# Half-range Fourier sums, one silu activation and accumulated weight sums in a gated attention block

## The chip, the cores and the metric

The kernel runs on one core of a Trainium2 chip. A NeuronCore has TensorE (PE, matrix products), VectorE (DVE), ScalarE (ACT), GpSimd (POOL) and SyncE (SP); every engine runs its own instructions in order and they wait for each other by semaphores. The metric is device time in microseconds: the median over the runs shown. For the kernel before, three runs gave a median of 1290.94 us (1290.84 to 1290.96).

## The reference

One layer over 512 latent tokens of width 2048, with 256 context tokens. The input is normalised and modulated, one projection `h @ w_in` (2048 to 9216 columns) gives q, k, v, the gates and the Fourier branch, and two mixers run side by side: attention, and a Fourier mix over four groups of 128 channels. What the change touches is this:

```python
u_b = p_rest[..., R_UB:R_ZB]          # 512 tokens x 512 channels
z_b = p_rest[..., R_ZB:R_GA]
ug = u.astype(jnp.float32).reshape(b, n, N_FNET_GROUPS, FNET_GROUP)
y = jnp.fft.fftn(ug, axes=(1, 3), norm="ortho").real     # tokens and 128 channels of a group
y_b = (_fourier_mix(u_b) * jax.nn.silu(z_b)) @ w_pb
```

`norm="ortho"` divides by the root of 512 x 128, which is 256. The result is the real part of a two-dimensional transform: with A the token transform of a group, it is a sum over channels of cos times the real part of A and a sum over channels of sin times its imaginary part, for each of 512 token frequencies. Because `u` is real, frequency 512 - f of A is the conjugate of frequency f.

## The kernel before

**Stages.** Three stages matter here. The start stage projects the 1024 columns of `u_b` and `z_b` while the modulation vectors come in. The Fourier stage, a dozen microseconds long, mixes `u_b` and multiplies by silu(`z_b`) into the tile `part`. After it come eight groups of the large projection, written as Strassen-like products, seven products to a group and four pieces to a product (`PRODUCTS`, `stream_product`, `Group`). Attention, the two branch projections and the output projection follow.

**How an f32 product is done.** Each f32 operand is split into a high part, rounded to fp32r by an ACT copy (`split_from`, L180), and a low part, the difference, by a DVE subtraction (L181). `mm3` (L338 to L340) multiplies high by high, high by low and low by high.

**The Fourier stage.** `halves` folds the tokens so that even and odd frequencies need only 256 rows each. `tokens(g)` (L918) forms, for one group of channels, the token transform of the frequencies 0 to 256: two parts e (even and odd frequencies) of six matmuls with 258 and 256 columns, their sums in `bank()`, split into `ah` and `al`. `positions(g)` (L931) then transforms the channels: for two halves q of the 512 frequencies and for cos and sin (r), that is four steps, each with a product against the high and the low part of the table `fch` on `ah` and one against its high part on `al`. The second half reads the same columns backwards (`slice(256, 0, -1)`) with the other sign of sin, for which `fch` has a third block. One DVE instruction (L944) scales by 1/256 and multiplies by the gated z. `gate_b(g)` (L946) makes silu(z) before it: a sigmoid on ACT (L949) into a tile `e` of one buffer, and a DVE product (L950).

**Order.** In this stage PE's order is written out (`ordered`, a manual schedule): tokens 0, tokens 1, positions 0, tokens 2, positions 1, tokens 3, positions 2, positions 3, then the first group. The order of the other engines, POOL and SP included, is chosen by the tile framework from its own cost model as instructions become ready; between instructions that are ready, those written earlier in the program go first in the places looked at below. An exception is written out: the splits of the next pieces (`split_piece` at L961) come behind `low[g]`, the last low part of that group of channels, on DVE.

**PSUM.** The pool of the start and Fourier stages has eight banks: two by `bank3()` (banks 0 and 1, `pc` in the trace), two by `bank2()` (banks 2 and 3, `pd`), four by `bank()` (banks 4 to 7, `pb`). The pool of the groups takes their place: the first tile `x`, which product P1 of group 0 sums into, lies over banks 0 and 1. A tile of the new pool waits for the last reader of the banks below it.

**Weights of the groups.** A product multiplies a sum of weight blocks. `chain[pc]` (tiles R0 to R3, one for each piece) holds a running sum: product P1 uses block 0, Q5 block 0 plus block 1, Q6 that plus block 2, Q4 that plus block 3. A block is added in one of two ways. It can be loaded by SP into one of the raw buffers `wr` and be added by DVE (L268): the steps named in `BY_DVE_GATES`, here step 1, that is Q5's. Or POOL issues an accumulating transfer from DRAM onto the tile, after the split of the sum before (`nxt`, L291). The sum is split two to four pieces ahead of its use (`look`). A piece takes a raw buffer for each block that it loads; there are four, and two more from L890 on.

POOL's queue around the stage holds the two stores of `part` to `b_d` (L966), the second of which waits for the last group of channels, the load `qr<-rot_d` (L1394), which waits until both stores have landed, and then the accumulating transfers of group 0.

**Who reads `part`.** `b_d` is read back much later, in the attention stage.

Of the kernel before, what the change touches and what calls it, by code (L numbers as in the profile page):

```python
# [10 lines left out]
F32 = mybir.dt.float32  # L11
F32R = mybir.dt.float32r
ACT = mybir.ActivationFunctionType
ALU = mybir.AluOpType
# [4 lines left out]
P = 128  # L19
D = 2048  # L20
T = 512
# [23 lines left out]
RAW = 4  # L45

HL, MORE_HL = 3, 2
EVEN = 258

# [9 lines left out]
BY_DVE_GATES, BY_DVE_OUT = (1,), ()  # L61
# [61 lines left out]
def block_kernel(ctx, tc, xT, ctx_rows, ctx_toks, x, c_row, w_ss, w_gate, vecs, qkg, rope, dft_c, dft_s,  # L123
                 w_start, w_g, w_pab, w_o, final_g, out):
    nc = tc.nc
# [30 lines left out]
    def uid(s):  # L156
        cnt[0] += 1
        return f"{s}{cnt[0]}"
# [11 lines left out]
    def bank(shape=(P, 512)):  # L170
        return ps.tile(list(shape), F32, tag="b1", bufs=4, name=uid("pb"))

    def bank2():
        return ps.tile([P, 512], F32, tag="b2", bufs=2, name=uid("pd"))
# [4 lines left out]
    def split_from(src, hi, lo):  # L179
        first = nc.scalar.activation(hi, src, ACT.Copy)  # L180
        return first, nc.vector.tensor_tensor(lo, src, hi.bitcast(F32), op=ALU.subtract)  # L181
# [16 lines left out]
    def stream(key, src, *a, **k):  # L198
        todo.append(Piece(key, src if isinstance(src, list) else [src], *a, **k))
# [136 lines left out]
    def mm3(o, ah, al, bh, bl, start, stop, cont=False):  # L336

        nc.tensor.matmul(o, ah, bh, start=start, stop=False, skip_group_check=cont)  # L338
        nc.tensor.matmul(o, ah, bl, start=False, stop=False, skip_group_check=cont)  # L339
        nc.tensor.matmul(o, al, bh, start=False, stop=stop, skip_group_check=cont)  # L340
# [25 lines left out]

    for p in start_pieces():
        if p[2:5:2] == (KK - 4, 0):
            stream(("dfts", 0), dft_s[:, : 2 * EVEN], 2 * EVEN, 2, "raw")
            stream(("dftc", 0), dft_c, 3 * P, 1, "raw")  # L370
        elif p[2:5:2] == (KK - 4, 4):
            stream(("dfts", 1), dft_s[:, 2 * EVEN :], T, 2, "raw")
        stream(("start", p), w_start[p[0] : p[0] + P * p[1]].rearrange("(p c) -> p c", p=P), p[1], p[2 + 1])
    kept = {}

# [15 lines left out]
    def stream_product(name, g, w, by_dve, pieces=4):  # L391

        what = next(p[2] for p in PRODUCTS if p[0] == name)
        for pc in range(pieces):
            key = (name, g, pc)
            part = lambda i: w[CHAIN[i][0], CHAIN[i][1], pc]
            r = (pc + CHAIN_FROM.get(g, 0)) % 4
            if isinstance(what, tuple) and name == "P7" and g >= BRANCH_A:
                stream(key, [p7_d[g - BRANCH_A, pc]], 1024, 2, pc=r)
            elif isinstance(what, tuple):  # L400
                off = name == "P7"
                stream(key, [w[a, b, pc] for a, b in what], 1024, 2, pc=r, nxt=part(3) if off else None, off=off)
            else:
                stream(key, [part(what)] if what in by_dve else [], 1024, 2, stage=what, pc=r,
                       nxt=part(what + 1) if what < (3 if g >= BRANCH_A else 2) and what + 1 not in by_dve else None)
                todo[-1].first = part(0)
# [14 lines left out]
    for g in range(LAST + 1):  # L421
        for name in ONE_GROUP:
            if (g, name) == (LAST, "Q4"):
                stream_keys(0)
            if g == KV:
                f = CTX_FORMS.index(next(f for n, f, _, _ in PRODUCTS if n == name))
                stream(("cf", name), cf_d[:, :, f].rearrange("i p j c -> p i j c"), 1024, 8, dst=ctx_tiles)
            stream_product(name, g, w_g[g], BY_DVE_GATES)
            for pc in range(4):
                p = context_piece(g, name, pc)  # L430
                if p:
                    src, cols = (ctx_toks[p[1]], 1024) if p[0] == "cn" else (ctx_rows[p[1]], 4 * C)
                    stream(p, src, cols, 1, "raw")
                    todo.insert(len(todo) - 4 + pc, todo.pop())
            for pc in range(4):
                if (g, name, pc) in GATE_AT:
                    q = GATE_AT[g, name, pc]
                    stream(("gate", q), w_gate[q], 1024, 1, "raw")
                    e = todo.pop()
                    at = next(i for i, x in enumerate(todo) if x.key == (name, g, pc))  # L440
                    todo.insert(at + 1, e)
    for i in range(2):
        stream(("b", i), flat(b_d[i]), 1024, 2, dst=lambda: tiles("b"))
    q = NGATE
# [19 lines left out]
    pst, ppool = region("part", "right")  # L464
    part = ppool.tile([P, NS, T], F32, name="part")
# [47 lines left out]
    with tc.issue_after(nc.scalar.activation(ce, cvt, ACT.Exp, scale=-1.0).ins):  # L513
# [3 lines left out]
    nc.vector.tensor_tensor(c2[:, :, 0:2].rearrange("p k j -> p j k"),  # L517
                            cvt.rearrange("p (j k) -> p j k", j=2),
                            ce.rearrange("p (j k) -> p j k", j=2), op=ALU.mult)
    fch = ppool.tile([P, 2, 3 * P], F32R, name="fch")  # L520
    fsq = [ppool.tile([P, 2, 2, EVEN], F32R, name="fsq0")]
    rx = pap.tile([P, T], F32, name="rx")
    wacc = bank3()
    def warm(n, src):
# [251 lines left out]
    with tc.manual_schedule(engines={E.PE}):  # L776
# [6 lines left out]
        with tc.manual_schedule(engines={E.Activation, E.DVE}):  # L783
# [25 lines left out]
            for kb in range(1, 4):  # L809
                k = kb + 1  # L810
# [32 lines left out]
            for kb in range(4, KK - 4, 2):  # L843
# [6 lines left out]
                k = kb + 2  # L850
# [42 lines left out]
    fn, fnp = region("fn")  # L893
    uh = fnp.tile([P, 2, 2, T], F32R, name="uh")
    ul = fnp.tile([P, 2, 2, T], F32R, name="ul")
    fsq.append(fnp.tile([P, 2, 2, 256], F32R, name="fsq1"))
    split_table(1)

    def halves(a):
# [16 lines left out]
    AH, low = {}, {}  # L916

    def tokens(g):  # L918

        ah, al = (fnp.tile([P, 2, 257], F32R, tag=n, bufs=2, name=uid(n)) for n in ("ah", "al"))  # L920
        c = slice(P * g, P * g + P)
        for e in range(2):
            n = fsq[e].shape[-1]
            acc = bank()
            for a in range(2):
                mm3(acc[:, :n], uh[:, a, e, c], ul[:, a, e, c], fsq[e][:, 0, a, :], fsq[e][:, 1, a, :], a == 0, a == 1)
            k = slice(e, 257 - e, 2)
            low[g] = split_from(acc[:, :n].rearrange("p (r f) -> p r f", r=2), ah[:, :, k], al[:, :, k])[1]
        AH[g] = ah, al

    def positions(g):  # L931

        ah, al = AH.pop(g)
        acc = bank2()
        steps = [(256 * q, P * (r and 1 + q), (slice(0, 256) if q == 0 else slice(256, 0, -1)), r)
                 for q in range(2) for r in range(2)]
        for n, (o, t, k, r) in enumerate(steps):
            for m, i in enumerate((0, 1)):
                nc.tensor.matmul(acc[:, o : o + 256], fch[:, i, t : t + P], ah[:, r, k], start=n == m == 0, stop=False,
                                 skip_group_check=True)  # L940
        for n, (o, t, k, r) in enumerate(steps):
            nc.tensor.matmul(acc[:, o : o + 256], fch[:, 0, t : t + P], al[:, r, k], start=False, stop=n == 3,
                             skip_group_check=True)
        nc.vector.scalar_tensor_tensor(part[:, 4 + g, :], acc, 1.0 / 256.0, part[:, 4 + g, :], op0=ALU.mult, op1=ALU.mult)  # L944

    def gate_b(g):  # L946
        z = part[:, 4 + g, :]
        e = fnp.tile([P, T], F32, tag="sil", bufs=1, name=uid("e"))
        nc.scalar.activation(e, z, ACT.Sigmoid)  # L949
        nc.vector.tensor_tensor(z, z, e, op=ALU.mult)  # L950

    tokens(0)
    tokens(1)
# [724 lines left out]
    for i in range(NSTEP + 3):  # L1678
        h, t = divmod(i, 4)
# [20 lines left out]
        n = next((n for n, at in enumerate(SUM_AT) if at <= i < at + 3), None)  # L1700
# [8 lines left out]
        if i == 3:  # L1709
            with tc.issue_after(maxima[0].ins), tc.issue_after(maxima[1].ins):  # L1710
                e = take((1024,))
# [8 lines left out]
        if i in GATE_STEPS:  # L1720
            n = NGATE + GATE_STEPS.index(i)
# [267 lines left out]
def _constants():  # L1989
    pos = np.arange(T)  # L1990
    inv = (THETA ** (-np.arange(32, dtype=np.float64) / 32)).astype(np.float32)
    ang = np.stack([(pos // GRID).astype(np.float32)[:, None] * inv,
                    (pos % GRID).astype(np.float32)[:, None] * inv], axis=1)
    ang = ang.astype(np.float64)
    cos, sin = np.cos(ang), np.sin(ang)
    cos = np.stack([cos, cos], axis=2).reshape(T, HD)
    sin = np.stack([-sin, sin], axis=2).reshape(T, HD)
    rope = np.stack([cos, sin]).reshape(2, 4, P, HD).transpose(2, 0, 1, 3).astype(np.float32)
    a = 2 * np.pi * (np.outer(np.arange(P), np.arange(P)) % P) / P
    dft_c = np.concatenate([np.cos(a), -np.sin(a), np.sin(a)], axis=1).astype(np.float32)  # L2000

    def table(f):
        a = 2 * np.pi * (np.outer(np.arange(T // 2), f) % T) / T
        v = np.concatenate([np.cos(a), np.sin(a)], axis=1).astype(np.float32)
        return v.reshape(2, P, -1).transpose(1, 0, 2).reshape(P, -1)

    dft_s = np.concatenate([table(np.arange(0, T // 2 + 1, 2)), table(np.arange(1, T // 2, 2))], axis=1)
    return np.ascontiguousarray(rope), np.ascontiguousarray(dft_c), np.ascontiguousarray(dft_s)


# [58 lines left out]
```

## Time and profile before

| | |
|---|---|
| median of three runs | 1290.94 us |
| the profiled execution | 1290.61 us, of which the span of instructions is 1288.8 us |
| PE, DVE, ACT, POOL busy in the span | 1272.9, 994.7, 682.2, 170.8 us |
| Fourier stage on PE (first token matmul to P1's first) | 144.60 to 156.13 us |
| P1 of group 0 on PE, 48 matmuls | 156.13 to 167.02 us |
| mean granted TensorE clock | 0.998 |

The profile counts microseconds from the start of the span. A timeline row gives start, duration (us), engine, line, operation, output and inputs, shape and count, and in brackets how long the engine sat idle before it and what released it. Matmuls overlap: a row's duration is longer than the distance to the next row's start, and that distance is what a matmul costs. The same holds for DVE and ACT, where one instruction's start to the next one's is a little shorter than its duration. A row of the stretches gives its length and then each engine's busy time and instruction count, the granted clock, the DMA share and GB/s.

### The profile page before, as it was taken

How to read it: one execution, taken by the hardware profiler on the slowest of the kernel's cores; microseconds unless marked ns; L12 is line 12 of the kernel's file. 1: busy time of each engine (PE TensorE's matmuls, PEld its weight loads, DVE VectorE, ACT ScalarE, POOL GpSimd, SP SyncE). 2: the span in 40 equal slices, each digit the busy share in tenths (PEclk: the TensorE clock that was granted, in tenths of full speed). 3: DMA queues.
4: the chain of work that ended last, by engine and by line, in shares of the span. 5: the costliest groups of instructions: out<-in, count | busy, mean ns of one | idle time of the engine just before them, and what ended most of it. 6: DMA issues, size and time to landing. Idle time of an engine off the chain costs nothing.

```text
span 1288.8 us, 17680 instructions
## 1 busy us (share of the span) xinstructions
PE 1272.9 (99%) x6586; PEld 1047.9 (81%) x6586; DVE 994.7 (77%) x1305; ACT 682.2 (53%) x1073; POOL 170.8 (13%) x222
## 2 busy tenths in 40 slices
PE   8999999999999999999999999999999999999997
PEld 5677887888888888888888888888888888888886
DVE  5767899889779787658587666788898777887677
ACT  5322654645556555444355544666667646464544
POOL 0000011111102011012031010012100211211210
PEclk9999999999999999999999999999999999999999
DMA  9998588888988988977879897578852989998986
GB/s 378 408 369 344 208 216 248 237 218 261 227 302 236 301 269 260 291 197 184 278 207 259 286 249 237 182 245 241 270 178 75 249 244 258 244 211 229 225 200 179
DMA packets 104486, 319.14 MB, mean 248 GB/s; under 512 B 9904, under 2 KB 33072, under 8 KB 100432
## 3 DMA queue, kind: packets, MB, share of 16 engines
q1 hardware_dynamic: 55056, 197.40, 42.3%
q0 software_dynamic: 27024, 98.19, 35.6%
q10 hardware_dynamic: 22320, 22.42, 5.1%
q8 instruction: 51, 0.84, 0.3%
q14 instruction: 35, 0.29, 0.1%
HBM read 283.36 MB, written 34.61 MB: 247 GB/s over the span
## 4 chain that ended last, share of the span: by engine, by line
PE 91%; DVE 3%; DMA 2%; ACT 2%; issue 1%; SPq 0%; ACTq 0%; DVEq 0%
PE banks L338 10%; PE banks L339 10%; PE banks L340 10%; PE x L340 9%; PE x L338 9%; PE x L339 9%; PE y L340 7%; PE y L339 7%; PE y L338 7%; PE banks L1543 2%; PE pd L566 2%; PE pb L338 1%; PE pb L339 1%; PE pb L340 1%; PE pc L338 1%; DMA wa<-in_w_ss 1%
## 5 line engine op out<-in xcount | busy, mean ns | idle before, releaser
L180 ACT ACTIVATE whi<-R 128x1024 fp32r<-128x1024 f32 x138 | 145.6, 1060 | 142.1 <-PE banks L340 55.3
L181 DVE TENSOR_TENSOR wlo<-R,whi 128x1024 fp32r<-128x1024 f32 x138 | 167.9, 1222 | 57.9 <-ACT whi L180 57.6
L181 DVE TENSOR_TENSOR wlo<-wr,whi 128x1024 fp32r<-128x1024 f32 (+1 forms) x122 | 147.2, 1214 | 63.1 <-ACT whi L180 63.1
L180 ACT ACTIVATE whi<-wr 128x1024 fp32r<-128x1024 f32 (+1 forms) x122 | 127.4, 1052 | 127.3 <-PE y L340 44.3
L338 PE MATMUL banks<-whi,s 128*128 128x512 f32 (+1 forms) x400 | 157.8, 394 | 0.9 <-DVE ev L1106 0.9
L339 PE MATMUL banks<-wlo,s 128*128 128x512 f32 (+1 forms) x400 | 155.8, 389 | 0.0
L340 PE MATMUL banks<-whi,s 128*128 128x512 f32 (+1 forms) x400 | 155.8, 389 | 0.0
L338 PE MATMUL x<-whi,s 128*128 128x512 f32 x352 | 137.1, 390 | 0.0
L340 PE MATMUL x<-whi,s 128*128 128x512 f32 x352 | 137.0, 389 | 0.0
L339 PE MATMUL x<-wlo,s 128*128 128x512 f32 x352 | 136.9, 389 | 0.0
L338 PE MATMUL y<-whi,s 128*128 128x512 f32 x316 | 123.1, 389 | 0.2 <-DVE cxe L1266 0.2
L339 PE MATMUL y<-wlo,s 128*128 128x512 f32 x316 | 123.1, 390 | 0.0
L340 PE MATMUL y<-whi,s 128*128 128x512 f32 x316 | 122.8, 389 | 0.0
L291 POOL DMA_DIRECT2D R<-in_w_g x64 | 56.0, 875 | 415.2 <-DVE wlo L181 212.6
L180 ACT ACTIVATE s<-wr 128x512 fp32r<-128x512 f32 (+2 forms) x93 | 60.9, 678 | 68.1 <-DMA wr<-cf_d 24.9
L338 PEld LDWEIGHTS banks<-whi,s 128*128 128x128 f32 x400 | 75.2, 188 | 16.6 <-DVE ev L1106 1.3
L181 DVE TENSOR_TENSOR s<-wr,s 128x512 fp32r<-128x512 f32 (+2 forms) x93 | 66.7, 750 | 28.3 <-ACT s L180 27.5
L340 PEld LDWEIGHTS banks<-whi,s 128*128 128x128 f32 x400 | 75.1, 188 | 15.3
L339 PEld LDWEIGHTS banks<-wlo,s 128*128 128x128 f32 x400 | 75.2, 188 | 13.6 <-DVE wlo L181 0.2
L340 PEld LDWEIGHTS x<-whi,s 128*128 128x128 f32 x352 | 66.1, 188 | 13.8
L339 PEld LDWEIGHTS x<-wlo,s 128*128 128x128 f32 x352 | 66.1, 188 | 13.7
L338 PEld LDWEIGHTS x<-whi,s 128*128 128x128 f32 x352 | 66.1, 188 | 13.6
(322 smaller groups left out, 2803.2 us busy)
## 6 DMA issues: line engine op xcount, KB each, us to landing
wr<-in_w_g SPq DMA_DIRECT2D x128, 512.0 KB, 5.8
R<-in_w_g POOLq DMA_DIRECT2D x64, 512.0 KB, 7.3
wa<-in_w_ss SPq DMA_DIRECT2D x31, 1024.0 KB, 9.7
R<-in_w_g SPq DMA_DIRECT2D x32, 512.0 KB, 6.0
wr<-in_w_gate SPq DMA_DIRECT2D x32, 512.0 KB, 5.1
wr<-in_w_o SPq DMA_DIRECT2D x24, 512.0 KB, 7.5
R<-in_w_o POOLq DMA_DIRECT2D x24, 512.0 KB, 9.2
wr<-in_w_pab SPq DMA_DIRECT2D x20, 512.0 KB, 6.0
```

Of the source, the lines that this page charges most:

```text
L180: first = nc.scalar.activation(hi, src, ACT.Copy)
L181: return first, nc.vector.tensor_tensor(lo, src, hi.bitcast(F32), op=ALU.subtract)
L291: nc.gpsimd.dma_start(chain[e.pc], e.nxt, accum_op=ALU.add)
L338: nc.tensor.matmul(o, ah, bh, start=start, stop=False, skip_group_check=cont)
L339: nc.tensor.matmul(o, ah, bl, start=False, stop=False, skip_group_check=cont)
L340: nc.tensor.matmul(o, al, bh, start=False, stop=stop, skip_group_check=cont)
L566: nc.tensor.matmul(acc[32 * j : 32 * j + 32], c2[:, n, :], w[:, k, :], start=n < 4, stop=n >= KK - 4)
L1543: nc.tensor.transpose(tp[:, k * P : (k + 1) * P], p[:, k * P : (k + 1) * P], ident)
```

## The change

There are three edits.

1. `positions(g)` forms the cosine and the sine sum for frequencies 0 to 256 only (258 columns with a pad), each by one `mm3` into a bank of its own: cosine into `bank2()`, sine into `bank3()`. ACT copies the sine sum to SBUF (`odd`). DVE writes `y`: cosine minus sine for frequencies 0 to 256, cosine plus sine, read backwards, for 257 to 511; a third DVE instruction multiplies by z. The factor 1/256 goes into the table, whose third block goes. The odd frequencies' token table gets 258 columns as well, so `ah` and `al` are 258 wide. Six matmuls to a group of channels take the place of twelve, four instructions (one on ACT, three on DVE) the place of one.
2. `gate_b` is one ACT activation, `Silu`, in place. The DVE product L950 and the tile `e` go. Every later gate of the kernel still uses `Sigmoid` (L1182) or `Tanh` (L1224, L1357).
3. For group 0 alone, `by_dve` is empty: block 1 of Q5's four sums is not loaded into raw buffers and added by DVE, but added by four accumulating transfers, each issued by POOL after the split of P1's piece.

```diff
-    fch = ppool.tile([P, 2, 3 * P], F32R, name="fch")
+    fch = ppool.tile([P, 2, 2 * P], F32R, name="fch")
...
-            stream_product(name, g, w_g[g], BY_DVE_GATES)
+            stream_product(name, g, w_g[g], BY_DVE_GATES if g else ())
...
 def tokens(g):
-            n = fsq[e].shape[-1]
-            acc = bank()
+            acc = bank()[:, :FREQ]
...
 def positions(g):
-        acc = bank2()
-        steps = [(256 * q, P * (r and 1 + q), (slice(0, 256) if q == 0 else slice(256, 0, -1)), r)
-                 for q in range(2) for r in range(2)]
-        for n, (o, t, k, r) in enumerate(steps):
-            for m, i in enumerate((0, 1)):
-                nc.tensor.matmul(acc[:, o : o + 256], fch[:, i, t : t + P], ah[:, r, k], start=n == m == 0, stop=False,
-                                 skip_group_check=True)
-        for n, (o, t, k, r) in enumerate(steps):
-            nc.tensor.matmul(acc[:, o : o + 256], fch[:, 0, t : t + P], al[:, r, k], start=False, stop=n == 3,
-                             skip_group_check=True)
-        nc.vector.scalar_tensor_tensor(part[:, 4 + g, :], acc, 1.0 / 256.0, part[:, 4 + g, :], op0=ALU.mult, op1=ALU.mult)
+        acc = [b()[:, :FREQ] for b in (bank2, bank3)]
+        for r, o in enumerate(acc):
+            t = slice(P * r, P * r + P)
+            mm3(o, fch[:, 0, t], fch[:, 1, t], ah[:, r, :], al[:, r, :], True, True)
+        z = part[:, 4 + g, :]
+        y, odd = (fnp.tile([P, n], F32, tag=t, bufs=2, name=uid(t)) for t, n in (("y", T), ("odd", FREQ)))
+        nc.scalar.copy(odd, acc[1])
+        nc.vector.tensor_tensor(y[:, :257], acc[0][:, :257], odd[:, :257], op=ALU.subtract)
+        nc.vector.tensor_tensor(y[:, 257:], acc[0][:, 255:0:-1], odd[:, 255:0:-1], op=ALU.add)
+        nc.vector.tensor_tensor(z, y, z, op=ALU.mult)

     def gate_b(g):
         z = part[:, 4 + g, :]
-        e = fnp.tile([P, T], F32, tag="sil", bufs=1, name=uid("e"))
-        nc.scalar.activation(e, z, ACT.Sigmoid)
-        nc.vector.tensor_tensor(z, z, e, op=ALU.mult)
+        nc.scalar.activation(z, z, ACT.Silu)
...
-    dft_c = np.concatenate([np.cos(a), -np.sin(a), np.sin(a)], axis=1).astype(np.float32)
+    dft_c = (np.concatenate([np.cos(a), np.sin(a)], axis=1) / 256.0).astype(np.float32)
...
-    dft_s = np.concatenate([table(np.arange(0, T // 2 + 1, 2)), table(np.arange(1, T // 2, 2))], axis=1)
+    dft_s = np.concatenate([table(np.arange(e, FREQ, 2)) for e in range(2)], axis=1)
```

`FREQ` is the new name of `EVEN`, 258.

More of the change, by code (lines that the diff above doesn't have):

```diff
@@ L47 @@
 HL, MORE_HL = 3, 2
-EVEN = 258
+FREQ = 258
 FORMS = ("Z5", "S2", "S3", "S4")
@@ L368, in block_kernel @@
         if p[2:5:2] == (KK - 4, 0):
-            stream(("dfts", 0), dft_s[:, : 2 * EVEN], 2 * EVEN, 2, "raw")
-            stream(("dftc", 0), dft_c, 3 * P, 1, "raw")
+            stream(("dfts", 0), dft_s[:, : 2 * FREQ], 2 * FREQ, 2, "raw")
+            stream(("dftc", 0), dft_c, 2 * P, 1, "raw")
         elif p[2:5:2] == (KK - 4, 4):
-            stream(("dfts", 1), dft_s[:, 2 * EVEN :], T, 2, "raw")
+            stream(("dfts", 1), dft_s[:, 2 * FREQ :], 2 * FREQ, 2, "raw")
         stream(("start", p), w_start[p[0] : p[0] + P * p[1]].rearrange("(p c) -> p c", p=P), p[1], p[2 + 1])
@@ L519, in block_kernel @@
                             ce.rearrange("p (j k) -> p j k", j=2), op=ALU.mult)
-    fch = ppool.tile([P, 2, 3 * P], F32R, name="fch")
-    fsq = [ppool.tile([P, 2, 2, EVEN], F32R, name="fsq0")]
+    fch = ppool.tile([P, 2, 2 * P], F32R, name="fch")
+    fsq = [ppool.tile([P, 2, 2, FREQ], F32R, name="fsq0")]
     rx = pap.tile([P, T], F32, name="rx")
@@ L895, in block_kernel @@
     ul = fnp.tile([P, 2, 2, T], F32R, name="ul")
-    fsq.append(fnp.tile([P, 2, 2, 256], F32R, name="fsq1"))
+    fsq.append(fnp.tile([P, 2, 2, FREQ], F32R, name="fsq1"))
     split_table(1)
@@ L918, in tokens @@
     def tokens(g):
-        ah, al = (fnp.tile([P, 2, 257], F32R, tag=n, bufs=2, name=uid(n)) for n in ("ah", "al"))
+        ah, al = (fnp.tile([P, 2, FREQ], F32R, tag=n, bufs=2, name=uid(n)) for n in ("ah", "al"))
         c = slice(P * g, P * g + P)
         for e in range(2):
-            n = fsq[e].shape[-1]
-            acc = bank()
+            acc = bank()[:, :FREQ]
             for a in range(2):
-                mm3(acc[:, :n], uh[:, a, e, c], ul[:, a, e, c], fsq[e][:, 0, a, :], fsq[e][:, 1, a, :], a == 0, a == 1)
-            k = slice(e, 257 - e, 2)
-            low[g] = split_from(acc[:, :n].rearrange("p (r f) -> p r f", r=2), ah[:, :, k], al[:, :, k])[1]
+                mm3(acc, uh[:, a, e, c], ul[:, a, e, c], fsq[e][:, 0, a, :], fsq[e][:, 1, a, :], a == 0, a == 1)
+            k = slice(e, FREQ, 2)
+            low[g] = split_from(acc.rearrange("p (r f) -> p r f", r=2), ah[:, :, k], al[:, :, k])[1]
         AH[g] = ah, al
```

## The prediction

> **What bounds the kernel now.** The page's first section comes first, then the stretches around the edits, then PE's waits.
>
> ```profile
> PE 1272.9 (99%) x6586; PEld 1047.9 (81%) x6586; DVE 994.7 (77%) x1305; ACT 682.2 (53%) x1073; POOL 170.8 (13%) x222
> ```
>
> ```profile
> 144.60:156.13 11.53, 11.53 (x98) 11.53 (x96) 11.25 (x21) 8.51 (x16) 0.53 (x1) 1.00 0.20 79
> 156.13:184.00 27.87, 27.87 (x124) 22.82 (x123) 27.87 (x31) 16.46 (x19) 4.58 (x6) 1.00 0.88 247
> 184.00:212.00 28.00, 27.29 (x120) 22.27 (x120) 27.93 (x37) 14.41 (x32) 5.93 (x7) 1.00 0.71 170
> 420.00:500.00 80.00, 80.00 (x357) 66.29 (x356) 63.67 (x103) 44.16 (x64) 6.88 (x8) 1.00 0.89 281
> ```
>
> ```profile
> PE x L339 <- DVE s L181: 0.7, 1, 0.7
> PE y L340 <- DVE s L181: 0.2, 1, 0.2
> ```
>
> PE is the bound nearly everywhere, so time that PE gives up in one place is won at the end if nothing else is late afterwards. But from the Fourier stage to 212 us DVE has no idle time either: two bounds lie on top of each other, and PE's only waits in groups 0 and 1 are these two, 0.9 us, both on DVE. An edit that shortens PE alone there would be eaten by DVE; so both are summed.
>
> **Edit 1 on PE.** The stage's PE timeline:
>
> ```profile
> 144.60 0.28 PE L338 MATMUL pb<-fsq,uh 128*128 128x258 f32 x1
> 147.47 1.12 PE L939 MATMUL pd<-ah,fch 128*128 128x256 f32 x8
> 148.43 0.64 PE L942 MATMUL pd<-al,fch 128*128 128x256 f32 x4
> 148.91 0.28 PE L338 MATMUL pb<-fsq,uh 128*128 128x258 f32 x1
> 153.12 0.28 PE L340 MATMUL pb<-fsq,ul 128*128 128x256 f32 x1
> 153.24 1.12 PE L939 MATMUL pd<-ah,fch 128*128 128x256 f32 x8
> 155.64 0.65 PE L942 MATMUL pd<-al,fch 128*128 128x256 f32 x4
> 156.13 0.40 PE L338 MATMUL x<-whi,s 128*128 128x512 f32 x1
> 167.02 0.39 PE L338 MATMUL y<-whi,s 128*128 128x512 f32 x1
> ```
>
> Twelve position matmuls take 148.91 - 147.47 = 1.44 us, 0.12 each, whether 256 or 258 columns. Six fewer in each of four groups of channels are 24 x 0.12 = 2.88 us: by count P1 starts at 153.25. The two more columns in the odd tables cost under 0.02 us each time, taken as nothing.
>
> The stage can't keep that whole, because the sums must be split before they are used. The rows that set the pace:
>
> ```profile
> 153.44 0.41 ACT L180 ACTIVATE ah<-pb 128x256 fp32r<-128x256 f32 x1 [0.30 <-PE pb L340]
> 153.74 2.00 ACT L180 ACTIVATE s<-Z 128x1024 fp32r<-128x1024 f32 x2
> 148.53 1.22 DVE L181 TENSOR_TENSOR wlo<-R,whi 128x1024 fp32r<-128x1024 f32 x1
> 149.66 0.69 DVE L944 SCALAR_TENSOR_TENSOR part<-pd,part 128x512 f32<-128x512 f32 x1
> 150.27 0.43 DVE L181 TENSOR_TENSOR al<-pb,ah 128x258 fp32r<-128x258 f32 x1
> 150.62 0.68 DVE L950 TENSOR_TENSOR part<-part,e 128x512 f32<-128x512 f32 x1
> 151.22 0.42 DVE L181 TENSOR_TENSOR al<-pb,ah 128x256 fp32r<-128x256 f32 x1
> ```
>
> From the starts, DVE pays 1.13 us for a weight's low part, 0.35 for `al`, 0.60 for L944 or L950. The new instructions are not in the trace. The half-width subtraction and addition read PSUM and one SBUF tile, as `al` does: 0.35 each; the one read backwards could cost more, and the bound taken for it is the 0.60 of a full width. The last product is like L950, 0.60. So positions costs DVE 1.30 us for 0.60. The copy `odd` is taken as `ah`'s 0.40 on ACT; Silu in place of Sigmoid as no difference there.
>
> Now DVE in order. Up to 148.5 nothing moves, since tokens 0 and 1 run as before. Then: low weight part 0 to 149.6, positions 0's three to 150.9, `al` 2 (two parts) to 151.6, positions 1's three to 152.9, `al` 3 to 153.6. PE would be at positions 3 at 152.5; its second matmul waits for `al` 3 until about 153.7, and five at 0.12 put its last start at 154.2. Before, `ah` started 0.32 us after the last token matmul's start (153.12 to 153.44); `odd` 3 so runs from 154.5 to 154.9. P1's first tile lies over the banks that `odd` 3 reads, so **P1 waits for that copy** and starts at 155.0, or up to 0.9 later if ACT is in one of its 1.0 us splits (`s<-Z` above). I take 155.1: PE gains 1.0 of the 2.88. The bounds are 153.25 (all hidden) and 156.7 (two backward reads at 0.60, and a low weight part of 1.13 ahead of `al` 3).
>
> **Edits 1 to 3 on DVE.** The additions that edit 3 removes, and what edits 1 and 2 exchange:
>
> ```profile
> 155.96 1.22 DVE L268 TENSOR_TENSOR R<-R,wr 128x1024 f32<-128x1024 f32 x1
> 159.96 2.36 DVE L268 TENSOR_TENSOR R<-R,wr 128x1024 f32<-128x1024 f32 x2
> 162.30 1.23 DVE L181 TENSOR_TENSOR wlo<-R,whi 128x1024 fp32r<-128x1024 f32 x1
> 164.04 1.22 DVE L268 TENSOR_TENSOR R<-R,wr 128x1024 f32<-128x1024 f32 x1
> L944 DVE SCALAR_TENSOR_TENSOR part<-pd,part x4: 685/686/687, 149.7 to 157.1; 128x512 f32<-128x512 f32 x4
> L950 DVE TENSOR_TENSOR part<-part,e x4: 683/690/693, 140.4 to 150.6; 128x512 f32<-128x512 f32 x4
> ```
>
> Four L268 at 1.14 give 4.5 us back. L950 gives 4 x 0.60 (three of them inside the crowded stretch), L944 another 2.4; the new instructions take 4 x 1.30 = 5.2. From 144.6 on DVE is 4.5 + 1.8 + 2.4 - 5.2 = 3.5 us earlier, PE 1.0. DVE's lead over PE so grows by 2.5 us, more than the 0.9 us of its two waits: those go. **Sum: 1.0 + 0.9 = 1.9 us**, 1290.6 - 1.9 = 1288.7 for the profiled execution; that one lies 0.33 under the median of 1290.94, so **1289.0 us** for the median. Later PE hardly waits (80.00 of 80.00 us busy in the stretch from 420, 99% in all), so I carry the gain to the end.
>
> **Edit 3 on POOL and the queues.**
>
> ```profile
> DMA to landing us min/median/max: 5.5/8.8/11.5
> DMA to landing us min/median/max: 2.9/3.4/3.8
> 158.07 0.53 POOL L966 DMA_DIRECT2D b_d<-part  x1 [3.88 <-DVE part L944]
> 162.48 0.55 POOL L1394 DMA_DIRECT2D qr<-rot_d  x1 [3.87 <-ACT whi L180]
> 166.70 0.90 POOL L291 DMA_DIRECT2D R<-in_w_g  x1 [3.68 <-DVE wlo L181]
> q1 hardware_dynamic: 55056, 197.40, 42.3%
> q0 software_dynamic: 27024, 98.19, 35.6%
> ```
>
> The first row is the landing of the accumulating transfers between 156 and 190 us, the second that of the stores to `b_d`. Four more issues of 0.9 us go to a POOL that is 13% busy. Per MB, q0 costs the DMA engines 35.6/98.19 against q1's 42.3/197.40, 1.7 times as much; the first three transfers start at 149.6 to about 158.5, mostly where the DMA share is 0.20 and the old loads stood still, and SP's raw buffers are free for the next product, so I put no cost there. Deadlines: P1 runs 10.89 us and a piece 2.72, so Q5's four pieces are due at 166.0, 168.7, 171.4 and 174.2, each less 2.3 for its split. The third, issued near 158.5, lands at 167.3 at the median (due 169.1). The fourth needs P1's last split (162.30 in the row above; about 160 after) and may stand on POOL behind the store of the last `part` and `rot_d`, which waits for its landing: issue 160 to 162.5, landing to 171.3, due 171.9. Covered, but not by much.
>
> **Edit 2's table load.**
>
> ```profile
> 137.35 1.06 ACT L180 ACTIVATE whi<-R 128x1024 fp32r<-128x1024 f32 x1 [2.46 <-DMA R<-in_w_g]
> 138.43 1.28 ACT L949 ACT_TABLE_LOAD   x1
> L1182 ACT ACTIVATE ev<-x x4: 1011/1030/1032, 419.2 to 763.2; 128x1024 f32<-128x1024 f32 x4
> L1224 ACT ACTIVATE x<-ev x3: 1012/1030/1031, 214.9 to 369.1; 128x1024 f32<-128x1024 f32 x3
> ```
>
> Today's load at L949 also serves the later Tanh and Sigmoid lines, which have none. With Silu there, zero to two loads may appear, at 214.9 or 419.2, each 1.28 us of ACT. ACT is idle 36 of 80 us in the stretch from 420, and no PE wait on ACT stands there: I take one load and no cost; uncovered, it is 1.3 us.
>
> The Trainium skill, page "ScalarE: Activation LUTs", section "What ACT_TABLE_LOAD costs", speaks against an extra set: a switch costs about 2.66 us there, the load and a drain of 1.38 us. The trace shows no drain: the ACTIVATE ahead of L949's load ends at 137.35 + 1.06 = 138.41, and the load starts at 138.43. Uncovered and by that page, the sum would be 1289.0 + 2.7 = 1291.7; by the row 1290.3.
>
> **Rivals.**
> - *The cut shows nearly whole*: DVE takes `al` 3 ahead of the products by z, ACT takes `odd` 3 at once. For it: the framework lets ready work pass work that waits for its predecessor. Against: DVE has no gap. P1 then starts at 153.25 to 154.4: 1287.2 to 1288.4, taken as 1287.7.
> - *DVE eats it*: P1 at 156.1 to 156.7 by the upper bound above, or the waits of 0.9 us stay because the forms after P1 are late for another reason. Gain 0 to 1.2: 1290.4.
> - *Slower: the fourth accumulation is late.* Its issue at 163.5 (today's end of that split) and the longest landing, 11.5, give 175.0, and 2.3 more for the split 177.3, against 174.2: PE stands 3.1 us at Q5's last piece, and the chain's next addition is as late. 1289.0 + 3.1 = 1292.1. With that issue it costs from a landing of 8.4 us and beats the gain from 10.3. Against: the wait of 3.1 needs the late issue and the worst row together.
>
> **How the numbers follow.** Forecast (gain 1.2 to 2.6) 0.50; nearly whole 0.27; eaten 0.18; late 0.05. The likeliest is 1289.0. Leaving out the ends of the first and last cases gives 1287.3 to 1290.7. A measurement of this kernel can tell about 0.2%, 2.6 us. Faster by that is the second case and a little of the first: 0.29; slower 0.05; within, 0.66.
>
> **What would show it.** PE's timeline: 24 matmuls fewer and P1's first `x` at 155.1, with a wait on ACT `odd`, or on `al` just ahead. DVE: L268 28 times instead of 32. PE's waits: the 0.7 and 0.2 gone. A new wait of PE at Q5, or of ACT on DMA `R`, would show the last rival. The forecast is wrong if P1 starts before 154.4 or after 155.8, or if the gain at P1 is lost by 212 us.

## The result and the profile after

The changed kernel takes 1293.16 us, the median of 22 runs (1290.13 to 1295.01), against 1290.95 of the kernel before, also 22 runs (1290.59 to 1293.65). The ratio is 1.0014 with a 95% interval of 1.0008 to 1.0020. That is slower, since the interval leaves 1 out, if by less than the 0.2% that the prediction took as its bound; it is 4.2 us above the forecast and outside the range. Its profiled execution took 1291.59 us, with a span of 1289.8. The granted clock was 0.997 in it.

The first section of the changed kernel's page, then the three stretches that answer to the first three shown of before (length, then busy time and count of PE, weight load, DVE, ACT and POOL; clock, DMA share, GB/s):

```profile
PE 1269.8 (98%) x6562; PEld 1044.8 (81%) x6562; DVE 990.7 (77%) x1305; ACT 684.1 (53%) x1078; POOL 172.9 (13%) x226
```

```profile
144.63:155.32 10.69, 9.36 (x74) 8.80 (x72) 10.25 (x22) 6.71 (x17) 1.44 (x2) 1.00 0.68 182
155.32:184.00 28.68, 26.52 (x114) 21.43 (x115) 24.03 (x28) 16.92 (x17) 7.25 (x9) 1.00 0.86 188
184.00:212.00 28.00, 28.00 (x125) 23.19 (x124) 28.00 (x37) 14.64 (x31) 5.95 (x7) 1.00 0.83 203
```

PE does 3.1 us less work over the span, and the Fourier stage is 0.84 us shorter (10.69 against 11.53). But in the stretch behind it PE, which had been busy all the time, now stands 2.16 us of 28.68, and DVE stands 4.65. From 184 us on PE is full again. The waits of PE between 150 and 215 us, then the rows of its timeline where the stage ends, then those where the new wait lies:

```profile
PE y L338 <- ACT whi L180: 1.4, 1, 1.4
PE pd L339 <- DVE al L181: 0.8, 1, 0.8
PE y L339 <- DVE wlo L181: 0.8, 1, 0.8
PE x L338 <- ACT odd L939: 0.5, 1, 0.5
```

```profile
154.53 0.28 PE L340 MATMUL pc<-ah,fch 128*128 128x258 f32 x1
155.32 0.50 PE L338 MATMUL x<-whi,s 128*128 128x512 f32 x1 [0.51 <-ACT odd L939]
```

```profile
176.04 0.50 PE L338 MATMUL y<-whi,s 128*128 128x512 f32 x1 [1.40 <-ACT whi L180]
177.30 0.50 PE L339 MATMUL y<-wlo,s 128*128 128x512 f32 x1 [0.76 <-DVE wlo L181]
```

The two waits at `al` and `odd` are the stage's own, as forecast. The two at `y`, 1.40 and 0.76 us one behind the other, are Q5's last piece: its high part comes late, and its low part after that. The timelines of ACT and DVE lead back to the weight:

```profile
174.94 1.06 ACT L180 ACTIVATE whi<-R 128x1024 fp32r<-128x1024 f32 x1 [4.81 <-DMA R<-in_w_g]
```

```profile
160.86 1.22 DVE L181 TENSOR_TENSOR wlo<-R,whi 128x1024 fp32r<-128x1024 f32 x1
```

```profile
176.02 1.22 DVE L181 TENSOR_TENSOR wlo<-R,whi 128x1024 fp32r<-128x1024 f32 x1 [4.65 <-ACT whi L180]
```

ACT stands 4.81 us until an accumulating transfer into `R` has landed. P1's last low part, which had to be done before that transfer could be issued, ended at 162.1. So the transfer left much later than it could. The timeline of POOL, which issues it, and the time from issue to landing of the two stores to `b_d`:

```profile
150.57 0.89 POOL L291 DMA_DIRECT2D R<-in_w_g  x1 [71.09 <-ACT ah L180]
153.84 0.55 POOL L962 DMA_DIRECT2D b_d<-part  x1 [2.38 <-DVE part L942]
156.21 0.86 POOL L291 DMA_DIRECT2D R<-in_w_g  x1 [1.82 <-DVE wlo L181]
158.61 0.86 POOL L291 DMA_DIRECT2D R<-in_w_g  x1 [1.54 <-issue]
159.17 0.86 POOL L962 DMA_DIRECT2D b_d<-part  x1
166.49 0.56 POOL L1390 DMA_DIRECT2D qr<-rot_d  x1 [6.45 <-PE x L340]
167.03 2.72 POOL L291 DMA_DIRECT2D R<-in_w_g  x3
```

```profile
DMA to landing us min/median/max: 4.5/5.6/6.7
```

Three of Q5's four sums were issued at 150.57, 156.21 and 158.61. The fourth is the first of the three at 167.03, right behind the load of `rot_d`. That load waits for the landing of the second store, issued at 159.17, and the store landed after 6.7 us, where before it took at most 3.8: the accumulating transfers of edit 3 are ahead of it in the same software queue. The one issued just ahead of it, at 158.61, landed after 6.1 us, at 164.7, and the store 1.2 us behind it. (The row names a matmul as what released the load. In the program it waits for both stores too, because its target `qr` lies over the tile `part`; another execution's profile, shown at the last experiment, names the store.) POOL takes its instructions in order, so the fourth sum stood 4.9 us behind a load that nothing waits for yet, from 162.1 to 167.03.

So the account against before is: P1 starts 0.81 us earlier, the two old waits of 0.9 are gone, and 2.16 of new waiting come in, 0.45 us to the bad by idle time. A wait costs PE somewhat more than its idle time, so the starts of the products on PE tell it better. The changed kernel is 0.81 earlier when P1 starts, 0.70 earlier when Q5 starts, 1.79 later when P2 starts (179.93 against 178.14), and 0.25 later at 245 us (245.21 against 244.96): from 199.90 to 223.20 the kernel before lost 1.54 us in two products with waits, and this one lost nothing. The 0.25 stays until 619 us. A wait of 0.57 us there for DVE (the tile `cxe`), where before it is 0.21, and one of 0.18 at 663 bring it to about 1.0, and the end is 0.98 later.

### The profile page after: what moved, and what is told of

It is laid out like the page before. It is cut to its first block, busy times and chain, and to the rows that moved or that the text cites. A ratio compares the mean times of both kernels' runs of the same rounds, so it can differ in the third digit from the quotient of the medians.

```text
span 1289.8 us, 17650 instructions
## 1 busy us (share of the span) xinstructions
PE 1269.8 (98%) x6562; PEld 1044.8 (81%) x6562; DVE 990.7 (77%) x1305; ACT 684.1 (53%) x1078; POOL 172.9 (13%) x226
## 4 chain that ended last, share of the span: by engine, by line
PE 88%; DMA 4%; DVE 3%; ACT 2%; issue 1%; SPq 0%; POOL 0%; ACTq 0%; POOLq 0%; DVEq 0%
PE banks L338 10%; PE banks L339 10%; PE banks L340 10%; PE x L339 8%; PE x L340 8%; PE x L338 8%; PE y L339 7%; PE y L340 7%; PE y L338 7%; PE banks L1539 2%; PE pd L566 2%; PE pc L338 1%; PE pb L338 1%; PE pc L339 1%; DMA wa<-in_w_ss 1%
## 5 line engine op out<-in xcount | busy, mean ns | idle before, releaser
L291 POOL DMA_DIRECT2D R<-in_w_g x68 | 59.2, 887 | 485.3 <-DVE wlo L181 211.8
```

The source lines that it names most:

```text
L291: nc.gpsimd.dma_start(chain[e.pc], e.nxt, accum_op=ALU.add)
```

## The experiments

Three theories stand against each other. **Q**: the order of POOL's queue and the load's wait for a landing make the fourth transfer late. **D**: the accumulating transfers are slow by themselves. **S**: edits 1 and 2 cost more than they save, and the stall hides it. Each time is a median; the ratio is to runs of the kernel before that were made beside it (medians 1290.7, 1290.89, 1290.78 and 1290.32 us).

### The load behind the fourth sum

The changed kernel with one load issued later, behind R3's accumulating transfer on POOL:

```diff
...
-            nc.gpsimd.dma_start(chain[e.pc], e.nxt, accum_op=ALU.add)
+            ins = nc.gpsimd.dma_start(chain[e.pc], e.nxt, accum_op=ALU.add)
+            if e.key == ("P1", 0, 3):
+                added.append(ins)
...
-    nc.gpsimd.dma_start(turning, rot_d)
...
             if (g, name) == (0, "Q5"):
+                with tc.issue_after(added[0].ins):
+                    nc.gpsimd.dma_start(turning, rot_d)
```

> The changed kernel with one instruction moved in POOL's queue: the load qr<-rot_d is issued behind the fourth accumulating transfer of group 0 (R3) instead of ahead of it. Everything else as changed. Theory Q (queue order): in the changed kernel R3's addition, whose data is ready at 162.1 us, stands on POOL until 167.0 because the load ahead of it waits for the landing of the second store to b_d. Here it is issued at 162 to 163 and lands by 171; PE's waits of 1.4 and 0.8 us at Q5's last piece go, P1 still starts near 155.3, and the time is 1290.95 - 0.8 - 0.9 = about 1289.2 (1288.8 to 1289.9), 3 to 4 us under the changed kernel. Theory D (the transfer itself): accumulating transfers are slow because the DMA engines are shared with SP's loads, wherever they stand in the queue. Then R3 lands near 174 here too and the time stays at 1291.5 to 1293.5. Theory S (edits 1 and 2 cost the time): as D in the time, with no wait of PE on R3 gone.

Measured: **1288.55 us** (11 runs, 1287.83 to 1290.40), ratio 0.9985 (0.9976 to 0.9993), a little below the range that Q had named (1288.8 to 1289.9). POOL's timeline, and PE's waits from 140 to 260 us, of this kernel:

```profile
162.53 0.85 POOL L291 DMA_DIRECT2D R<-in_w_g  x1 [2.33 <-DVE wlo L181]
166.43 0.56 POOL L1416 DMA_DIRECT2D qr<-rot_d  x1 [3.05 <-PE x L341]
```

```profile
PE pd L341 <- DVE al L181: 0.8, 1, 0.8
PE x L340 <- ACT odd L941: 0.5, 1, 0.5
```

The fourth sum leaves at 162.53, 4.5 us earlier, and both waits at Q5 are gone. The load still goes at 166.43, as late as in the changed kernel, and nobody waits for it. At 245 us PE is 2.31 us ahead of the kernel before (242.65 against 244.96). D falls: the same four transfers cost nothing when the fourth is issued in time.

### Edits 1 and 2 without edit 3

```diff
-            stream_product(name, g, w_g[g], BY_DVE_GATES if g else ())
+            stream_product(name, g, w_g[g], BY_DVE_GATES)
```

> Edits 1 and 2 alone: edit 3 is undone, so Q5's sums of group 0 are added by DVE as before. Theories Q and D: no wait on an accumulating transfer before Q6. P1 starts near 155.3, but DVE has 1.0 us more work than before up to 212 us and the four additions are back, so DVE's two waits of 0.9 us grow to about 1.9 to 2.7 and take the gain at P1 back: 1290.5 to 1292.0. Theory S: the slow times are those of edits 1 and 2, 1292.5 to 1293.5, with the spread of 1290 to 1295 that the changed kernel's runs show.

Measured: **1293.16 us** (11 runs, 1292.43 to 1294.52), ratio 1.0014 (1.0005 to 1.0022), above the 1290.5 to 1292 that Q and D expected and inside the range of S. The stores' landing and the larger of PE's waits (140 to 260 us):

```profile
DMA to landing us min/median/max: 3.1/3.2/3.3
```

```profile
PE x L338 <- ACT s L180: 1.4, 1, 1.4
PE x L339 <- DVE wlo L181: 1.4, 1, 1.4
```

Without accumulating transfers ahead of them the stores land in 3.3 us, so the 6.7 are edit 3's doing. What holds PE here is in the main DVE, 206 to 215 us into the span: a wait of 1.4 on `wlo` at 206.32, one of 0.6 on DVE at 215.00, and between them one of 1.4 on ACT at 210.77, which had itself stood until 209.14 for PE's late product. By the terms of the prediction these two edits alone give DVE 5.2 - 2.4 - 1.8 = 1.0 us more work, and the first addition into `ev`, a fixed point of DVE's order, comes at 206.78 against 204.41 before, 2.4 us late: the 1.0, and most of the rest is 1.1 us of idling from 145.9 to 148.2, where DVE waits for `ah` (before, products of `gate_b` filled that time); this sum is an estimate from the two traces. So without edit 3 these two edits lose. S is no account of the changed kernel for all that, since the experiment above has them too, and wins.

### Edit 3 alone, on the kernel before

```diff
-            stream_product(name, g, w_g[g], BY_DVE_GATES)
+            stream_product(name, g, w_g[g], BY_DVE_GATES if g else ())
```

> Edit 3 alone, on the kernel before: the Fourier stage and the sigmoid as before. POOL's queue has the same order as in the changed kernel (rot_d ahead of R3's addition). Theories Q and D: P1 starts at 156.1, R3 is issued at 166 to 168 and lands at 173 to 177, PE stands 1 to 3 us at Q5's last piece, the DVE waits of 0.9 us go: 1291.0 to 1294.0, and single runs spread by 2 us or more. Theory S: edit 3 only relieves DVE, 1290.0, spread as small as before (0.5 us).

Measured: **1298.63 us** (6 runs, 1297.87 to 1302.13), ratio 1.0059 (1.0047 to 1.0071). Far above what was expected. PE's one wait, POOL's rows and DVE's:

```profile
PE y L339 <- DVE wlo L181: 7.8, 1, 7.8
```

```profile
157.49 0.56 POOL L966 DMA_DIRECT2D b_d<-part  x1
167.62 0.55 POOL L1394 DMA_DIRECT2D qr<-rot_d  x1 [9.56 <-PE x L340]
168.16 2.71 POOL L291 DMA_DIRECT2D R<-in_w_g  x3
```

```profile
178.15 1.23 DVE L276 TENSOR_TENSOR wr<-R,wr 128x1024 f32<-128x1024 f32 x1 [8.21 <-DMA R<-in_w_g]
179.29 2.36 DVE L181 TENSOR_TENSOR wlo<-R,whi 128x1024 fp32r<-128x1024 f32 x2
```

The same mechanism, one step further. The load of `rot_d` goes 10.1 us after the store, and the sums behind it at 168.16. The framework has put a difference for P7 (L276) ahead of Q5's last low part on DVE, and that difference needs one of the sums issued behind the load: DVE, in order, stands 8.21 us, and PE 7.8 behind it. One late load has so held POOL, DVE and PE in turn.

### Three accumulating transfers instead of four

The changed kernel with two lines more in `stream_product`, so that Q5's fourth sum is loaded and added by DVE again:

```diff
...
+            if (g, pc) == (0, 3):
+                by_dve = BY_DVE_GATES
```

> The changed kernel with three accumulating transfers in place of four: Q5's fourth sum of group 0 is loaded and added by DVE as before; rot_d's load keeps its place in POOL's queue, behind the store and ahead of Q6's additions. Theory Q: nothing that Q5 needs stands behind rot_d any more; P1 near 155.3, no PE wait at Q5, one L268 (1.1 us of DVE) back: 1289.0 to 1290.2. Theory D: the third transfer lands late instead and the time stays over 1291. Theory S: 1292 to 1293.5.

Measured: **1291.16 us** (11 runs, 1289.50 to 1292.55), ratio 1.0000 (0.9991 to 1.0009), where Q had expected 1289.0 to 1290.2. The time alone would fit D (over 1291), but no piece of Q5 waits any more, as Q says; there is another stall, earlier. PE's largest wait and the rows of DVE that make it:

```profile
PE x L339 <- DVE wlo L181: 2.1, 1, 2.1
```

```profile
161.66 2.35 DVE L181 TENSOR_TENSOR s<-S,s 128x1024 fp32r<-128x1024 f32 x2
163.93 1.21 DVE L181 TENSOR_TENSOR wlo<-R,whi 128x1024 fp32r<-128x1024 f32 x1
```

This is P1's last piece, whose low part stands behind `s<-S`. The experiments with the sigmoid, below, come back to it.

### The sine sum in a bank that P1 does not take

The first experiment's kernel with the sine sums in `bank()`:

```diff
-        acc = [b()[:, :FREQ] for b in (bank2, bank3)]
+        acc = [b()[:, :FREQ] for b in (bank2, bank)]
```

> The kernel with rot_d's load behind R3's addition, and the sine sum of positions in one of the four bank() banks (4 to 7) in place of bank3() (0 and 1), so that P1's first tile no longer lies over banks that the copy odd still reads. Theory: P1's wait on odd (0.5 us, and 0.8 us from positions' last matmul to P1's first) goes; P1 starts near 154.7 in place of 155.3, DVE's lead over PE (3.5 us at 204 us) covers it, and 0.6 us more is won: about 1288.0. Rival: DVE or the transfers have no more to give, the start moves and is given back by 212 us: 1288.5 as without it.

Measured: **1288.21 us** (10 runs, 1286.71 to 1288.84), ratio 0.9977 (0.9968 to 0.9986), the fastest of all. The end of the stage and P1's start on PE's timeline:

```profile
154.60 0.28 PE L342 MATMUL pb<-ah,fch 128*128 128x258 f32 x1
154.72 0.39 PE L340 MATMUL x<-whi,s 128*128 128x512 f32 x1
```

P1 follows 0.12 us after the stage's last matmul and waits for nothing: the 0.5 us for the copy `odd` are gone from the trace. In the medians it is 0.3 us, too little to be told apart from the first experiment's by these runs. The trace shows where the gain goes. PE is 0.88 us ahead of the first experiment's kernel from 177 to 616 us, and at 635 it is level with it (634.77 against 634.81): between them it waits for a result of DVE, the tile `cxe` of a later stage, for which the other kernel does not wait at all.

```profile
PE y L340 <- DVE cxe L1264: 0.5, 1, 0.5
```

### POOL's order kept, the wait for a landing taken away

The changed kernel with the tile `part` cut in two, u's half and z's half. `qr` then lies over u's half alone, which the stores do not read; the load of `rot_d` stays ahead of the fourth sum.

```diff
-    part = ppool.tile([P, NS, T], F32, name="part")
+    part = ppool.tile([P, 4, T], F32, name="part")
+    partz = ppool.tile([P, 4, T], F32, name="partz")
...
-        z = part[:, 4 + g, :]
+        z = partz[:, g, :]
...
-        nc.gpsimd.dma_start(b_d[i], part[:, 4 + 2 * i : 6 + 2 * i, :])
+        nc.gpsimd.dma_start(b_d[i], partz[:, 2 * i : 2 * i + 2, :])
```

> The changed kernel with POOL's queue in the changed kernel's order (store, rot_d's load, then R3's addition), but with the tile part cut into two tiles, one of the u sums and one of the z products. The buffer that rot_d's load fills lies over the u sums alone, so the load no longer waits for the landing of the stores. Theory Q in its narrow form (the wait for the landing holds the queue, not the load's place in it): R3 is issued near 162.5 and the time is that of the kernel with the load behind, 1288.6 (1288.2 to 1289.3). Rival: the load of 512 KB ahead of R3 in the one software queue delays its landing as well; R3 lands at 172 or later and the time is 1290 or more.

Measured: **1289.01 us** (11 runs, 1288.36 to 1291.46), ratio 0.9987 (0.9979 to 0.9996). POOL's timeline:

```profile
160.03 0.85 POOL L1391 DMA_DIRECT2D qr<-rot_d  x1
162.69 0.89 POOL L291 DMA_DIRECT2D R<-in_w_g  x1 [1.81 <-DVE wlo L181]
```

Of PE's waits only those for `al` and `odd` are left. The store lands as late as in the changed kernel (6.6 us), and it does no harm. So neither the load's place in the queue nor the store's late landing is the cause by itself: it is the wait for that landing, at the head of a queue in order.

### The sigmoid and its product again

The first experiment's kernel with edit 2 undone.

```diff
-        nc.scalar.activation(z, z, ACT.Silu)
+        e = fnp.tile([P, T], F32, tag="sil", bufs=1, name=uid("e"))
+        nc.scalar.activation(e, z, ACT.Sigmoid)
+        nc.vector.tensor_tensor(z, z, e, op=ALU.mult)
```

> The kernel with rot_d's load behind R3's addition and edit 2 undone: sigmoid on ACT and the product by z on DVE as before the change, with no extra table load. By the count in the prediction DVE pays 1.8 us for the three products inside the crowded stretch: DVE's lead falls from 3.5 to 1.7 us, still over what PE's 0.9 us of waits need, P1 starts 0.3 to 1.0 later: 1288.9 to 1289.6. Rival (from the trace of edits 1 and 2 alone, where DVE idled 1.1 us between 145.8 and 148.5 waiting for ah, just where these products stood): the products fit into idle time and the time stays at 1288.5.

Measured: **1292.44 us** (11 runs, 1291.21 to 1296.31), ratio 1.0014 (1.0005 to 1.0023): 3.9 us above the first experiment's kernel. Neither expectation holds, and the four products (4 x 0.60 = 2.4 us) are not that long. PE's largest wait, and DVE:

```profile
PE x L341 <- DVE wlo L181: 2.7, 1, 2.7
```

```profile
159.39 0.68 DVE L181 TENSOR_TENSOR s<-wr,s 128x512 fp32r<-128x512 f32 x1
159.99 2.35 DVE L181 TENSOR_TENSOR s<-Z,s 128x1024 fp32r<-128x1024 f32 x2
162.26 2.35 DVE L181 TENSOR_TENSOR s<-S,s 128x1024 fp32r<-128x1024 f32 x2
164.54 1.22 DVE L181 TENSOR_TENSOR wlo<-R,whi 128x1024 fp32r<-128x1024 f32 x1
```

P1's last low part starts at 164.54; in the first experiment's kernel it was 161.02:

```profile
161.02 1.22 DVE L181 TENSOR_TENSOR wlo<-R,whi 128x1024 fp32r<-128x1024 f32 x1
162.15 1.22 DVE L181 TENSOR_TENSOR s<-S,s 128x1024 fp32r<-128x1024 f32 x1
```

Of the 3.52 us, 0.60 are a product (the others fall where DVE had been idle or had done other splits), 0.60 an `s<-wr` that stood earlier there, and 2.27 the two `s<-S`, which there came behind the low part. They split the form for P7; between P1 and P7 stand three other products.

### That order put right, in two steps

Both are the kernel of the experiment before with one more edit. First the second half of Q5's form behind P1's last low part (`p1_last`):

```diff
+                    if (f, h) == ("Z5", 1):
+                        with tc.issue_after(p1_last[0].ins):
+                            self.forms[f][4 * h : 4 * h + 4] = split_form(whole[f, h])
-                    if ready:
+                    elif ready:
```

> e7_sigmoid once more (rot_d load behind R3, sigmoid and product), but the second half of Q5's form, s<-S (2 x 1.14 us on DVE), is issued behind the low part of P1's last piece. In e7 that low part started at 164.54, behind s<-S, and PE stood 2.7 us for it. If DVE's order is what edit 2 bought (theory O): the low part starts near 162.3, PE's wait falls from 2.7 to about 0.6 us, median 1290.3 (1289.7 to 1291.0). If the products by the sigmoid cost by their own length (theory W): the wait stays above 2 us and the median near 1292.4.

Measured: **1289.88 us** (11 runs, 1289.07 to 1291.07), ratio 0.9992 (0.9983 to 1.0001). The edit had moved one instruction, a half of Q5's form that the trace names `s<-Z`, and not the pair `s<-S` that its expectation named. PE's wait fell by that one's length, 1.14, though the median fell by 2.6:

```profile
PE x L343 <- DVE wlo L181: 1.6, 1, 1.6
```

Then the pair itself, with `if f == "S3":` in that condition:

> e7_sigmoid once more (rot_d load behind R3, sigmoid and product), and the two s<-S, which split the form for P7, three products later, are issued behind the low part of P1's last piece. e9_low_part_first had moved one instruction of 1.14 us, a half of Q5's form (shown as s<-Z, not the s<-S named in its expectation), and the wait fell by as much, 2.7 to 1.6 us. By theory O (DVE's order) the low part starts 2.27 us earlier than in e7, at 162.3, PE's wait falls from 2.7 to about 0.4 us, and the median to 1289.2 (1288.5 to 1290.2), within 1.5 us of e1_load_behind's 1288.55: then edit 2 was worth its order and little of its length. By theory W (the products by the sigmoid cost by their length) other work takes the place, the wait stays above 1.5 us and the median above 1291.

Measured: **1289.24 us** (11 runs, 1287.83 to 1289.58), ratio 0.9988 (0.9979 to 0.9997). DVE's rows and PE's wait:

```profile
162.63 1.21 DVE L181 TENSOR_TENSOR wlo<-R,whi 128x1024 fp32r<-128x1024 f32 x1
163.77 1.21 DVE L181 TENSOR_TENSOR s<-S,s 128x1024 fp32r<-128x1024 f32 x1
```

```profile
PE x L343 <- DVE wlo L181: 0.5, 1, 0.5
```

Theory O held, in the wait and in the time: by the medians, 3.2 of the 3.9 us that edit 2 seemed to bring came from an order of DVE that it had tipped. The 0.7 that remain lie within the noise of two medians. The traces show less of it: at 245 us PE of the first experiment's kernel is 1.95 us ahead of that with the sigmoid, and the pair's order gives back 1.39 of them. The rest of the 3.9 arises later (the profiled executions end 3.1 us apart) or in no trace, and its cause is not shown. With the three accumulating transfers the same pair stands in the same place; there its order was not changed, so that case rests on its rows alone.

### The changed kernel again

Unchanged, once more.

> The changed kernel itself, beside the two kernels that take the wait away, for a second profiled execution, since its first one (1291.59) was one of its fast ones and its median is 1293.2. Theory Q: wherever an execution is slower, the second store lands later, R3 is issued later, and PE's wait at Q5's last piece is longer by the same: for 1293.2, about 1.6 us more than the 2.2 us of the first. Rival: the wait at Q5 is 2.2 us again and the rest of the time is lost elsewhere.

Measured: **1293.09 us** (11 runs, 1291.90 to 1295.10), ratio 1.0020 (1.0011 to 1.0029). This profiled execution took 1292.36 us, 0.77 more than the one shown above, and the question was whether Q5's wait had grown. It had not: 1.3 and 0.8 us again. Here the profile names the store as the release:

```profile
166.54 0.56 POOL L1390 DMA_DIRECT2D qr<-rot_d  x1 [6.22 <-DMA b_d<-part]
```

So Q's expectation of a longer wait missed. **What stays open:** both profiled executions lie under the kernel's median, by 1.57 and 0.73 us, and no trace shows what the usual execution adds. The first experiment's kernel is 2.56 us ahead of the changed one at 245 us and 3.5 in its profiled execution, but 4.6 in the medians. What is added goes with a stall of PE at P1 or Q5: of the kernels with 2 us or more at one piece, the profiled executions lie 0.7 to 1.6 under the median; of the others they lie 0.5 under to 0.7 above it.

## Why the prediction was wrong

**The failed step is the cover of the fourth accumulating transfer.** The prediction had "issue 160 to 162.5, landing to 171.3, due 171.9. Covered, but not by much". It saw that the transfer stands behind the store and behind `rot_d`, which waits for the store's landing. But its latest issue, 162.5, is the load's own issue in the trace of before (162.48), where the store left at 158.07 and landed after 3.8 us. In the changed kernel the store left 1.1 us later (159.17), and since it stands behind transfers that edit 3 adds to the same queue, it landed after 6.7, 2.9 us more. So the load went at 166.49 and the fourth sum at 167.03 instead of 162.5 at the latest, the weight was there for its split at 174.94 instead of 171.3, and PE stood 2.16 us. An estimate from these rows: with the landing of before the load would have gone at 163.6 (3.8 us, and 0.6 from the landing to the load's issue, as in both traces) and the sum 0.5 later, to be there 7.8 us after that, at 171.9. That is the very time at which the prediction had it due. The old landing would just have been covered; the new one could not be.

**The rival that came true was priced nearly right for a wrong reason.** "The fourth accumulation is late" gave 1292.1, with a chance of 0.05, because it seemed to need the latest issue and the longest landing, 11.5, together. It needed no long landing: from 167.03 to the split at 174.94 are 7.9 us, less than the 8.8 of the median transfer in the prediction's row. And the issue was later than the 163.5 that was put as its end, since what sets it is a landing and not the split. The sign that the prediction named for it, a new wait of PE at Q5 and one of ACT on DMA `R`, is what the trace shows. The rival's wait was 3.1 us, the measured 2.16, and its median still too low by 1.1, which is the open rest.

**The gain was right in its sum, partly by luck.** With one load moved, the time is 1288.55 us against 1289.0 forecast, and by 245 us 2.31 us are won against 1.9. But the two terms of 1.0 and 0.9 are off in opposite ways. With the load moved, P1 starts 0.66 us earlier than before and ends 0.53 earlier, not 1.0. The waits are worth 1.78, not 0.9: a product that nothing holds takes 10.88 us, and three of before took 11.12, 11.88 and 11.42. The wait of 0.71 alone made its product 1.00 us longer, and the 0.24 at Q5 are in no row of waits. By the terms:

- *P1's start*: 155.1 forecast, 155.32 measured (155.47 with the load moved), in the forecast's own order: a wait on `al` (0.82), then one on `odd` (0.51). The last sine matmul began at 154.53, not 154.2. "Nearly whole" and "eaten" are out for the changed kernel.
- *New instructions*: the copy took 0.37 (0.40 put), the half-width ones stand 0.33 apart (0.35), the product 0.60. The bound of 0.60 for the backward read was not needed.
- *DVE 3.5 us earlier*: the addition into `ev` comes 3.54 us earlier (200.87 against 204.41) with the queue mended; in the changed kernel the 4.65 us of idling eat it (205.24).
- *The old waits of 0.7 and 0.2*: gone.
- *A cost of the transfers on the DMA engines*: none seen, with the fourth issued in time.

**Edit 2's table load** was one, at no cost, as taken. ACT's timeline where the first Sigmoid follows:

```profile
418.22 0.64 ACT L180 ACTIVATE s<-wr 128x512 fp32r<-128x512 f32 x1 [0.82 <-DVE wr L276]
418.87 1.28 ACT L1178 ACT_TABLE_LOAD   x1
```

Tanh, at 216.77 here, needs none. The drain of 1.38 us that the Trainium skill states (page "ScalarE: Activation LUTs", section "What ACT_TABLE_LOAD costs") isn't there, before as after: the activation ahead ends at 418.86. PE has no wait between 400 and 430 us.

**What the prediction's sum could not see** is that the three edits are not independent. Edits 1 and 2 alone lose (1293.16), edit 3 alone loses more (1298.63), the three lose (1293.16), and the three with the load moved win (1288.55). Edit 3 pays for what edit 1 puts on DVE; and DVE's order, which the framework chooses by its own estimates, tips with small amounts of work, so that by the medians 2.4 us of products taken away were worth 3.9, of which the traces show 1.95 by 245 us.

## What to carry to other kernels

When an edit adds transfers to a queue, look for everything already in that queue whose landing somebody waits for: a wait for a landing is priced with the landing under the new load, not with that of the old trace. An instruction that waits for a landing should not stand ahead of one that is due, on an engine that works in order; move it behind, or lay its target where nothing is being read. And when an edit on a saturated engine is worth more than the work it removes, look whether the order of that engine has changed: then the order can be had without the edit.

## What was not expected of the hardware

- A store of 512 KB from POOL landed 2.9 to 3.8 us after its issue with no accumulating transfer ahead of it, and after 4.4 to 9.6 us with one to three ahead. The second store landed 1.2 us behind the accumulating transfer issued just ahead of it in the changed kernel (165.9 against 164.7) as with edit 3 alone (167.0 against 165.8). That fits a queue in order; no run here sets it apart from transfers that share the DMA engines.
- DVE reads PSUM backwards as fast as forwards: 255 columns of `y` read backwards (L941) took 0.41 us, 257 read forwards (L940) 0.42, and the starts behind them are 0.33 and 0.34 apart.

```profile
149.93 0.42 DVE L940 TENSOR_TENSOR y<-pd,odd 128x257 f32<-128x257 f32 x1
150.27 0.41 DVE L941 TENSOR_TENSOR y<-pd,odd 128x255 f32<-128x255 f32 x1
```
